# Opening of a macaron transformer layer: fewer warming steps, transfers put behind the opening, and norm steps one pair later

## The chip, the core and the metric

The kernel runs on one core of one Trainium2 chip. The metric is the time of one execution on the device in microseconds (us): the median of three runs of the kernel before is 2084.44 us (2084.19 to 2086.21). The engines are named as the profile names them: PE (TensorE, matmuls), DVE (VectorE), ACT (ScalarE), POOL (GpSimd) and SP (SyncE, which here only issues transfers, each in its turn).

## The reference, cut to what matters

One layer of depth 1 over 1024 latent tokens and 256 context tokens of width 1024. Latent and context rows have their own modulation (nine vectors each, computed from `c` and `c_ctx`), and the same weights.

```python
m_l = jnp.split(silu(c) @ ada_w + ada_b, 9, axis=-1)
m_c = jnp.split(silu(c_ctx)[None] @ ada_w + ada_b, 9, axis=-1)
x   = x   + 0.5 * m_l[2] * swiglu(modulate(rms_norm(x, norm1_w), m_l[0], m_l[1]), w1, w3, w2)
ctx = ctx + 0.5 * m_c[2] * swiglu(modulate(rms_norm(ctx, norm1_w), m_c[0], m_c[1]), w1, w3, w2)
y_l, _ = token_mixing(modulate(rms_norm(x, norm2_w), m_l[3], m_l[4]),
                      modulate(rms_norm(ctx, norm2_w), m_c[3], m_c[4]), ...)
x = x + m_l[5] * y_l
x = x + 0.5 * m_l[8] * swiglu(modulate(rms_norm(x, norm3_w), m_l[6], m_l[7]), ffn2 weights)
return rms_norm(x, final_norm_w)
```

`swiglu` is `(silu(h @ w1) * (h @ w3)) @ w2` with a hidden width of 2816. The change touches the modulation, the first FFN of both streams, and the norm of the latents that follows it.

## The kernel before, in words

Activations lie with the channels on the 128 partitions, in tiles of 512 tokens (latents: groups 0 and 1) or 256 (context: group 2). Each matrix product is made of three fp32r matmuls: an operand is split into a rounded high part and the rest. For a weight tile `raw` the parts are `whi` (written by ACT) and `wlo` (written by DVE, raw minus whi); for activations `hh` and `hl`. In the products of the context FFN the weights are themselves in `hh`/`hl` slots and the hidden values `g` are split into `ghi` and `glo`.

**Opening.** `consts` loads small tables. Then `WARM` matmuls of 128x128 ones (L1970, fp32, each seen as two records) run on an idle psum tile while the first data comes in. After them a `Recorder` notes all work of the opening (context norm, latent norm, first FFN pair); `rec.run()` writes it out in an order that a list scheduler with its own costs finds. All its rows bear line L147. `pe_load(j, hold)` fetches a column group of the modulation's weights (512 KB, `ada<-in_adaN`) for sums on PE; for the very first (j of 8) `hold` makes DVE clear eight columns of the tile, and the transfer waits for that write. After the recorder, plain code follows: `cond_row` fetches the two condition rows (`condc`, and `c_ctx` into a tile named `ada1`, two halves each), ACT takes silu of them, and `mod_load` fetches the other 48 columns (`ada<-in_adaT`, 512 KB each), which DVE multiplies with the rows and reduces (72 reductions, L510) while the rest of the first FFN runs. The scheduler of the framework merges this code into the order of each engine by priority; nothing there ties the fetches on SP to the recorder's end. The silu steps are tied to the recorder's last ACT instruction already.

**Context pairs.** After the first FFN's latent part, `ctx_ffn` makes the second product of the context FFN in 11 pairs of hidden blocks (numbered 0 to 10 below). In pass p of its loop it fetches pair p+2 (`ctx_load`: two halves of `s<-cgd`, four weight tiles `s<-in_w`), splits pair p+1 (`ctx_split`: four hh on ACT, hl on DVE, one of them on POOL, then ghi and glo), makes the 48 matmuls of pair p into psb (`ctx_sums`; "sums p" below), and then takes one step off the list `norms`, which is the latents' second norm cut into steps: column sums of squares on PE (L570) and a power on POOL, the diagonals (`diag1`), the row product on PE and its copy to `nrb` on ACT (`rows1`, L2104), and one step for each of the norm columns (`norm1(k)`: nt on DVE, hh on ACT, hl on DVE; L603, L604, L615). In this region the order on every engine is the program's, into which only work from outside it (the `raw` tiles of the projection that follows, `whi<-raw`) is merged. Tiles of `s` and slots of hh/hl are reused in turn, so a transfer waits for the last reader of the buffer that it takes.

Of the kernel before, what the change touches and what calls it, by code (L numbers as in the profile page):

```python
# [17 lines left out]
P = 128  # L18
D = 1024
KD = D // P  # L20
# [17 lines left out]
SCHED = mybir.DependencyInfo(mybir.DependencyClass.NoSync, mybir.DependencyReason.SCHED_ONLY)  # L38
# [9 lines left out]
class View:  # L48
# [72 lines left out]
    def get(self):  # L121
        t = self.root.real
        for f in self.how:
            t = f(t)
        return t
# [279 lines left out]
class Trunk:  # L405
# [50 lines left out]
    def cond_row(self, name, tag=None):  # L456
        t = self.tile(self.dp, [P, D], F32, tag or "cond" + name)
        for o in (0, 512):
            self.nc.sync.dma_start(t[:, o:o + 512], self.I[name][:, o:o + 512].broadcast_to([P, 512]))
        return t  # L460

    def pe_cond(self, pool):
# [11 lines left out]
        nc.vector.scalar_tensor_tensor(out=self.ab1, in0=self.col("ada_b")[:, 8:16], scalar=1.0, in1=self.col("norm1_w"),  # L474
                                       op0=ALU.add, op1=ALU.mult)

    def pe_load(self, j, hold=False):
        t = self.ada_tile()
        if hold:
            self.nc.vector.memset(t[:, :8], 0.0)  # L480
        self.nc.sync.dma_start(t, self.I["adaN"][PECOL.index(j)])
        return t

# [13 lines left out]

    def mod_load(self, j):
        t = self.ada_tile()
        self.nc.sync.dma_start(t, self.I["adaT"][j])  # L500
        return t

    def mod_col(self, j, ctxs, early=False):
# [625 lines left out]
    def ctx_open(self, xp, n1):  # L1129
        nc, I = self.nc, self.I  # L1130
        a, b = self.mcol(1, 1), self.mcol(0, 1)
        cx = [self.tile(n1, [P, 4 * CTX], F32, f"cx{i}") for i in range(2)]
        for i in range(4):
            nc.sync.dma_start(cx[i // 2][:, i % 2 * 512:i % 2 * 512 + 512], I["ctxP"][:, i * 512:(i + 1) * 512])
        self.ada, self.ab, self.cur = -1, (0, 2, 3, 4, 1), {}
        cur, ws = self.cur, defaultdict(list)
        f32r = lambda pool, tag, bufs=1: tuple(self.tile(pool, [P, 512], F32R, t, bufs) for t in tag)
        slots = iter([*(f"0{k}" for k in range(KD)), *(f"1{k}" for k in range(4, KD))])
        fresh = iter(range(NW))
        raws = iter(range(2 * NW))  # L1140

        def dst(i, q):
            if not q and i < 6:
                return f32r(self.wp, ("whi", "wlo"), NH)
            if not q and i < 11:
                return f32r(self.fp, ("s", "s"), self.ns)
            s = next(slots, None)
            if s:
                return self.hslot(s)
            n = next(fresh)  # L1150
            return f32r(xp, (f"x1{2 * n}", f"x1{2 * n + 1}")) if n < 4 else f32r(self.fp, ("s", "s"), self.ns)

        def half(i, q):
            n = next(raws)
            src = (self.w1, self.w3)[i % 2][i // 2][:, 512 * q:512 * q + 512]
            if n % 2:
                raw = self.tile(xp, [P, 512], F32, f"x0{n // 2 % 8}")
                nc.sync.dma_start(raw, src)
            else:
                raw = self.raw_half(src)  # L1160
            ws[i].append(self.half(raw, dst(i, q)))

        def load(k):
            for j in (8 + k, k):
                cur[j] = self.pe_load(j, j == 8)

        rb = self.ctx_norm(cx, n1, lambda: load(0))
        self.h[2] = []
        hs = [self.hslot(f"1{k}") for k in range(4)]
        csum = lambda n: self.tile(n1, [P, n], F32, "csum", 2)  # L1170

        def norm(k):
            t = cx[k // 4][:, k % 4 * CTX:(k % 4 + 1) * CTX]
            hi, lo = (x[:, k % 2 * CTX:(k % 2 + 1) * CTX] for x in hs[k // 2])
            nc.vector.scalar_tensor_tensor(out=t, in0=t, scalar=a[:, k:k + 1], in1=rb, op0=ALU.mult, op1=ALU.mult)
            nc.scalar.activation(hi, t, AF.Identity, bias=b[:, k:k + 1])
            nc.vector.scalar_tensor_tensor(out=lo, in0=t, scalar=b[:, k:k + 1], in1=hi.bitcast(F32), op0=ALU.add, op1=ALU.subtract)
            self.h[2].append((hi, lo))

        def cols(k):  # L1180
            js = (8 + k, k)
            if k == 0:
                for j in js:
                    p = self.psB()
                    self.col_out(j, self.col_sums(p, 0, j, csum(2 * P)[:, :P], p, P))
                return
            for i, j in enumerate(js):
                self.pe_sums(pc, i * P, cur.pop(j))
            sm = csum(2 * P)
            nc.scalar.copy(sm, pc[:, :2 * P])  # L1190
            src = [self.pe_turn(pc, 2 * P + 2 * i, sm[:, i * P:(i + 1) * P]) for i in range(2)]
            for j, p in zip(js, src):
                self.col_out(j, p)

        cols(0), norm(0)
        pc = self.psB()
        for s in OPEN:
            if isinstance(s, tuple):
                half(*s)
            elif s > 0:  # L1200
                load(s)
            else:
                cols(-s), norm(-s)
        banks = [self.psA() for _ in range(4)] + [self.psB() for _ in range(NW // 2 - 4)]
        acc = [banks[i // 2][:, i % 2 * CTX:(i % 2 + 1) * CTX] for i in range(NW)]
        for k in range(KD):
            for i in range(NW):
                w, h = self.wslice(ws[i], k), self.h[2][k]
                for j, (u, v) in enumerate(((0, 0), (1, 0), (0, 1))):
                    nc.tensor.matmul(acc[i], w[u], h[v], start=k + j == 0 and i % 2 == 0, stop=k == KD - 1 and j == 2,  # L1210
                                     skip_group_check=True)
        return acc
# [730 lines left out]
    def run(self):  # L1943
# [24 lines left out]
        idle = self.psA()  # L1968
        for _ in range(WARM):
            nc.tensor.matmul(idle[:, :P], self.ones, self.ones, start=True, stop=True)  # L1970
        rec = Recorder(self, 0.0, 345e3, 2.0, False)
# [20 lines left out]
        self.h = {tg: get(self.h[tg]) for tg in LATTG}  # L1992
        self.T = [get(t) for t in self.T]
        self.tp = tp.real
        self.cs = [self.cond_row("c"), self.cond_row("c_ctx", "ada1")]
        for t in self.cs:
            for o in (0, 512):
                x = nc.scalar.activation(t[:, o:o + 512], t[:, o:o + 512], AF.Silu)
# [31 lines left out]
        def norm_step(tg, i, a, b):  # L2030
            with self.low(NLOW if tg == 1 and i in (1, 2) else None):
                norm_part(tg, i, a, b)
# [18 lines left out]
        norm2 = lambda tg, i: norm_step(tg, i, self.mcol(4, int(tg == 2)), self.mcol(3, int(tg == 2)))  # L2051
# [33 lines left out]
        def spill(tg):  # L2085
            o = TGS[tg][0]
            for k in range(KD):
                self.nc.sync.dma_start(self.xd[k * P:(k + 1) * P, o:o + 512], self.x[tg][k])
# [4 lines left out]
        def norm1(k):  # L2093
            self.h[1].append(self.hslot(f"1{k}"))
            norm2(1, 3 + k)
# [8 lines left out]
            nc.scalar.copy(nrm[1], pr)  # L2104

        dg = []
        norms = [lambda: norm2(1, 1), diag1, rows1] + [lambda k=k: norm1(k) for k in range(KD - 1)]
        with tc.manual_schedule(engines={mybir.EngineType.PE, mybir.EngineType.DVE, mybir.EngineType.Activation,
                                         mybir.EngineType.Pool, mybir.EngineType.SP}):
            self.ctx_ffn(norms)  # L2110
        norm1(KD - 1)
        spill(1)
        self.lg_start(n2)
        self.psN = self.psB
# [2 lines left out]
        rec = Recorder(self)  # L2117
# [31 lines left out]
        for tg in LATTG:  # L2149
            o, n = TGS[tg]  # L2150
# [57 lines left out]
NQ = 7  # L2208
MB = ((4, 5, 6, 7), (4, 5, 6, 7))
RPRI = 20  # L2210
WARM = 30
NW = 14
F0 = 2
BACKLOG = 3
# [105 lines left out]
```

## Time and profile before

| what | value |
|---|---|
| median of three runs | 2084.44 us |
| the profiled execution's own time | 2084.73 us |
| its span, first to last instruction | 2082.9 us |
| mean granted TensorE clock | 0.995 |
| PE busy | 2067.1 us, 99% |
| DVE, ACT, POOL busy | 1506.3, 987.2, 89.7 us |
| DMA moved | 374.26 MB, mean 180 GB/s |

Times inside the run are counted from the first instruction of the span. A row of the order in time has start, length, engine, line, operation, out<-in with its shape, how many are merged, and in brackets how long the engine was idle before it and what ended that. "PEclk" or "granted clock" is the share of full speed at which TensorE ran.

### The profile page before, as it was taken

The numbers are of one execution on the slowest core, as the hardware profiler recorded it, in microseconds if no ns is written. First come the engines' busy times: TensorE is split into PE (matmuls) and PEld (weight loads), VectorE is DVE, ScalarE is ACT, GpSimd is POOL, SyncE is SP. The second block draws the span as 40 slices with busy tenths as digits, with TensorE's granted clock in tenths as the row PEclk, the third lists the DMA queues.
The fourth block names the chain that finished last, engine by engine and source line by source line (L and its number), as shares of the span: only waits on it lengthen the run. The fifth ranks groups of instructions, "written<-read, shape, count | busy, mean of one in ns | idle before, by whom it ended". The sixth has DMA issues, their size and how long they took to land.

```text
span 2082.9 us, 34381 instructions
## 1 busy us (share of the span) xinstructions
PE 2067.1 (99%) x12438; PEld 1768.0 (85%) x12438; DVE 1506.3 (72%) x2732; ACT 987.2 (47%) x1828; POOL 89.7 (4%) x118
## 2 busy tenths in 40 slices
PE   9999999999999999999999999999999999999998
PEld 8998888888888889998888988888888888888888
DVE  5789999976665688765676478767776666765686
ACT  4665343343444446565575246444434334344553
POOL 0000000000000012001021001000000000010000
PEclk9999999999999999999999999999999999999999
DMA  9863766744488785574232233242344444477674
GB/s 351 276 202 109 248 228 226 267 148 151 142 288 276 268 286 197 175 221 127 80 116 90 82 87 109 88 162 82 112 157 146 146 163 149 159 239 227 219 241 148
DMA packets 207131, 374.26 MB, mean 180 GB/s; under 512 B 23921, under 2 KB 42225, under 8 KB 206833
## 3 DMA queue, kind: packets, MB, share of 16 engines
q1 hardware_dynamic: 206672, 371.94, 53.8%
q8 instruction: 97, 1.59, 0.3%
q14 instruction: 74, 0.60, 0.1%
q10 hardware_dynamic: 288, 0.13, 0.0%
HBM read 293.46 MB, written 70.12 MB: 175 GB/s over the span
## 4 chain that ended last, share of the span: by engine, by line
PE 89%; DMA 5%; DVE 3%; ACT 1%; issue 1%; SPq 0%; DVEq 0%; POOLq 0%; ACTq 0%
PE psa L147 24%; PE psb L147 11%; PE psa L439 9%; PE psa L441 9%; PE psa L440 9%; PE psb L440 8%; PE psb L439 8%; PE psb L441 8%; DMA raw<-in_w 2%; DMA hl<-sd 1%; DMA hl<-in_w 1%; DMA s<-in_w 1%; DVE wlo L435 1%; DMA xd<-x 1%; PE psa L1970 0%
## 5 line engine op out<-in xcount | busy, mean ns | idle before, releaser
L434 ACT ACTIVATE whi<-raw 128x512 fp32r<-128x512 f32 x385 | 243.2, 632 | 552.4 <-issue 190.9
L435 DVE TENSOR_TENSOR wlo<-raw,whi 128x512 fp32r<-128x512 f32 x385 | 264.5, 688 | 209.1 <-ACT whi L434 207.4
L439 PE MATMUL psa<-hh,whi 128*128 128x512 f32 x676 | 263.4, 390 | 0.6 <-ACT s L731 0.6
L441 PE MATMUL psa<-hh,wlo 128*128 128x512 f32 x676 | 263.1, 389 | 0.0
L440 PE MATMUL psa<-hl,whi 128*128 128x512 f32 x676 | 263.0, 389 | 0.0
L147 PE MATMUL psa<-hh,wlo 128*128 128x512 f32 (+1 forms) x664 | 234.5, 353 | 2.3 <-DVE wlo L147 2.3
L147 PE MATMUL psa<-hh,whi 128*128 128x512 f32 (+1 forms) x664 | 234.8, 355 | 0.8 <-ACT hh L147 0.5
L147 PE MATMUL psa<-hl,whi 128*128 128x512 f32 (+1 forms) x664 | 234.1, 353 | 0.0
L440 PE MATMUL psb<-hl,whi 128*128 128x512 f32 x584 | 227.3, 389 | 0.3 <-DVE hl L435 0.3
L439 PE MATMUL psb<-hh,whi 128*128 128x512 f32 x584 | 227.3, 389 | 0.0
L441 PE MATMUL psb<-hh,wlo 128*128 128x512 f32 x584 | 227.2, 389 | 0.0
L147 DVE TENSOR_TENSOR wlo<-raw,whi 128x512 fp32r<-128x512 f32 (+1 forms) x217 | 139.1, 661 | 103.4 <-ACT whi L147 101.5
L147 ACT ACTIVATE whi<-raw 128x512 fp32r<-128x512 f32 (+1 forms) x217 | 129.6, 609 | 151.4 <-PE psa L147 110.5
L439 PEld LDWEIGHTS psa<-hh,whi 128*128 128x128 f32 x676 | 127.0, 188 | 27.1 <-ACT s L731 1.0
L441 PEld LDWEIGHTS psa<-hh,wlo 128*128 128x128 f32 x676 | 126.9, 188 | 26.4
L440 PEld LDWEIGHTS psa<-hl,whi 128*128 128x128 f32 x676 | 126.9, 188 | 26.1
L147 PEld LDWEIGHTS psa<-hh,wlo 128*128 128x128 f32 x664 | 127.2, 192 | 17.3 <-DVE wlo L147 2.5
L147 PEld LDWEIGHTS psa<-hh,whi 128*128 128x128 f32 x664 | 126.9, 191 | 17.6 <-issue 1.0
L147 PEld LDWEIGHTS psa<-hl,whi 128*128 128x128 f32 x664 | 127.1, 192 | 14.7 <-issue 0.2
L440 PEld LDWEIGHTS psb<-hl,whi 128*128 128x128 f32 x584 | 109.6, 188 | 23.2 <-DVE hl L435 0.6
L439 PEld LDWEIGHTS psb<-hh,whi 128*128 128x128 f32 x584 | 109.6, 188 | 23.1 <-ACT hh L434 0.3
L441 PEld LDWEIGHTS psb<-hh,wlo 128*128 128x128 f32 x584 | 109.6, 188 | 22.7
(469 smaller groups left out, 4347.1 us busy)
## 6 DMA issues: line engine op xcount, KB each, us to landing
raw<-in_w SPq DMA_DIRECT2D x316, 256.0 KB, 3.3
gd<-s SPq DMA_DIRECT2D x154, 256.0 KB, 2.9
s<-in_w SPq DMA_DIRECT2D x110, 256.0 KB, 4.5
ada<-in_adaT SPq DMA_DIRECT2D x48, 512.0 KB, 4.7
raw<-gd SPq DMA_DIRECT2D x91, 256.0 KB, 3.4
sd<-s SPq DMA_DIRECT2D x44, 256.0 KB, 2.7
raw<-sd SPq DMA_DIRECT2D x44, 256.0 KB, 3.1
hh<-in_w SPq DMA_DIRECT2D x44, 256.0 KB, 4.0
```

The source lines that it names most:

```text
L147: self.rec.add(self.eng, lambda: f(*map(get, a), **{x: get(v) for x, v in k.items()}), outs, ins, name, a, k)
L434: nc.scalar.activation(hi, src, AF.Copy)
L435: (eng or nc.vector).tensor_tensor(out=lo, in0=src, in1=hi.bitcast(F32), op=ALU.subtract)
L439: mm(ps, wa[0], xa[0], start=start, stop=False, skip_group_check=more)
L440: mm(ps, wa[0], xa[1], start=False, stop=False, skip_group_check=more)
L441: return mm(ps, wa[1], xa[0], start=False, stop=stop, skip_group_check=more)
```

## The change

Three things are changed.

1. `WARM` falls from 30 to 20, and `pe_load` has no `hold` any more: the first column's transfer waits for no write.
2. `cond_row` and `mod_load` tie each of their transfers to the last transfer that the recorder issued on SP (`self.last`): they come behind it in SP's order.
3. The list of norm steps gets an empty first step, and one norm column less; the last two columns are now made after the loop.

```diff
     def cond_row(self, name, tag=None):
...
-            self.nc.sync.dma_start(t[:, o:o + 512], self.I[name][:, o:o + 512].broadcast_to([P, 512]))
+            x = self.nc.sync.dma_start(t[:, o:o + 512], self.I[name][:, o:o + 512].broadcast_to([P, 512]))
+            self.tc.add_manual_dep(x.ins, self.last, SCHED, reason="order")
...
-    def pe_load(self, j, hold=False):
+    def pe_load(self, j):
         t = self.ada_tile()
-        if hold:
-            self.nc.vector.memset(t[:, :8], 0.0)
         self.nc.sync.dma_start(t, self.I["adaN"][PECOL.index(j)])
...
     def mod_load(self, j):
         t = self.ada_tile()
-        self.nc.sync.dma_start(t, self.I["adaT"][j])
+        x = self.nc.sync.dma_start(t, self.I["adaT"][j])
+        self.tc.add_manual_dep(x.ins, self.last, SCHED, reason="order")
...
-                cur[j] = self.pe_load(j, j == 8)
+                cur[j] = self.pe_load(j)
...
         self.tp = tp.real
+        self.last = rec.last["SP"]
         self.cs = [self.cond_row("c"), self.cond_row("c_ctx", "ada1")]
...
-        norms = [lambda: norm2(1, 1), diag1, rows1] + [lambda k=k: norm1(k) for k in range(KD - 1)]
+        norms = [lambda: None, lambda: norm2(1, 1), diag1, rows1] + [lambda k=k: norm1(k) for k in range(KD - 2)]
...
             self.ctx_ffn(norms)
-        norm1(KD - 1)
+        norm1(KD - 2), norm1(KD - 1)
...
-WARM = 30
+WARM = 20
```

SP before, in the first FFN pass of the opening, from 90 us on: weight tiles (`raw<-in_w`), stores of context hidden values (`cgd<-s`), and between them a condition row and columns.

```order
L147 DMA raw_1314<-in_w 128x512
L147 DMA cgd<-s_1262 128x256
L459 DMA ada_542_2695<-in_c_ctx 128x512 x2
L500 DMA ada_632_3166<-in_adaT 128x1024
L147 DMA raw_1371<-in_w 128x512
L500 DMA ada_630_3160<-in_adaT 128x1024
L147 DMA cgd<-s_1369 128x256
L500 DMA ada_631_3163<-in_adaT 128x1024
L147 DMA raw_1436<-in_w 128x512
L147 DMA raw_1458<-in_w 128x512
```

SP now, at the end of the opening: behind its last store (`gd<-s`, the latents' hidden values) stand both condition rows, and then the columns.

```order
L147 DMA gd<-s_2455 128x512
L653 DMA raw_3002<-in_w 128x512
L147 DMA gd<-s_2676 128x512
L459 DMA condc_2681<-in_c 128x512 x2
L459 DMA ada_542_2684<-in_c_ctx 128x512 x2
L499 DMA ada_630_3149<-in_adaT 128x1024
L653 DMA raw_3004<-in_w 128x512
L499 DMA ada_631_3152<-in_adaT 128x1024
```

In the first place the weight tiles now follow each other with only the stores between; the moved ones go some 70 places down. PE before, at the end of sums 0 (`psb<-ghi`, `glo` with hh, hl) and the start of sums 1:

```order
L440 MATMUL psb_7842<-glo_7813,hh_1666_7788 128x256
L441 MATMUL psb_7842<-ghi_7812,hl_1667_7789 128x256
L570 MATMUL psa_7922<-ones_84,nacc_1621_7620 128x1 x4
L439 MATMUL psb_7839<-ghi_7870,hh_1687_7854 128x256
L440 MATMUL psb_7839<-glo_7871,hh_1687_7854 128x256
```

The same place now:

```order
L440 MATMUL psb_7831<-glo_7802,hh_1666_7777 128x256
L441 MATMUL psb_7831<-ghi_7801,hl_1667_7778 128x256
L439 MATMUL psb_7828<-ghi_7859,hh_1687_7843 128x256
L440 MATMUL psb_7828<-glo_7860,hh_1687_7843 128x256
L441 MATMUL psb_7828<-ghi_7859,hl_1688_7844 128x256
```

The four column sums of the norm (L570) have gone behind the 48 matmuls of sums 1. ACT before, from ghi of pair 3 on: the copy of the norm's row, the split of pair 4, then three weight tiles of the projection that follows.

```order
L434 ACTIVATE ghi_8044<-s_7934 128x512
L2104 COPY nrb_8101<-psa_8096 128x512
L434 ACTIVATE hh_1740_8114<-s_8017 128x512
L434 ACTIVATE hh_1742_8118<-s_8018 128x512
L434 ACTIVATE hh_1744_8122<-s_8019 128x512
L434 ACTIVATE hh_1746_8126<-s_8020 128x512
L434 ACTIVATE ghi_8130<-s_8021 128x512
L434 ACTIVATE whi_8747<-raw_8743 128x512
L434 ACTIVATE whi_8771<-raw_8767 128x512
L434 ACTIVATE whi_8890<-raw_8886 128x512
```

ACT now, from the same place (s_7998 to s_8002 are pair 4, s_8085 begins pair 5):

```order
L434 ACTIVATE ghi_8025<-s_7915 128x512
L434 ACTIVATE whi_8736<-raw_8732 128x512
L434 ACTIVATE whi_8760<-raw_8756 128x512
L434 ACTIVATE hh_1738_8096<-s_7998 128x512
L434 ACTIVATE hh_1740_8100<-s_7999 128x512
L434 ACTIVATE hh_1742_8104<-s_8000 128x512
L434 ACTIVATE hh_1744_8108<-s_8001 128x512
L434 ACTIVATE ghi_8112<-s_8002 128x512
L434 ACTIVATE whi_8879<-raw_8875 128x512
L2105 COPY nrb_8169<-psa_8164 128x512
L434 ACTIVATE hh_1755_8182<-s_8085 128x512
```

Two of the three weight tiles have come ahead of pair 4's split, and the third stands ahead of the copy of the row, which is now behind pair 4 and ahead of pair 5. SP now, around the transfer that fills that third tile (raw_8875); cgd and s_8341 to s_8343 are of pair 8, and the buffer of s_8343 is the one that pair 4's glo reads last:

```order
L985 DMA s_8345<-cgd 128x256 x2
L987 DMA s_8341<-in_w 128x512
L987 DMA s_8342<-in_w 128x512
L987 DMA s_8343<-in_w 128x512
L653 DMA raw_8875<-in_w 128x512
L653 DMA raw_8897<-gd 128x512
L653 DMA raw_8899<-in_w 128x512
```

Before, the like transfer (raw_8886) stood one place ahead of the fourth tile of pair 7; it has gone behind three tiles of pair 8, while the stores of the latents that stood ahead of the raw tiles (`xd<-x`, four of them) have gone behind them.

## The prediction

> **What bounds the kernel now.** I read the page's busy table first, then the list of who waited for whom on PE, then a table of stretches around each long wait, then the order of time on ACT, DVE and SP at three places.
>
> ```profile
> PE 2067.1 (99%) x12438; PEld 1768.0 (85%) x12438; DVE 1506.3 (72%) x2732; ACT 987.2 (47%) x1828; POOL 89.7 (4%) x118
> PE psa L147 <- DVE wlo L147: 2.3, 1, 2.3
> PE psa L1970 <- DVE ones L450: 1.0, 1, 1.0
> PE psa L570 <- DVE nacc L561: 1.0, 1, 1.0
> PE psb L440 <- DVE glo L435: 0.2, 1, 0.2
> ```
>
> PE is busy for 2067.1 of 2082.9 us, so only three things can move the time: the few waits of PE, the rate at which its clock runs, and work taken from it. The rows give a wait's total, how often it came, and the longest. The second costs nothing that the change touches; the other three lie in its reach. Next, the stretches (PE busy, matmuls in brackets, then other engines, granted clock, DMA share, GB/s):
>
> ```profile
> 104.90:107.30 2.40, 0.12 (x2) 0.06 (x1) 2.12 (x4) 2.40 (x6) 0.00 (x0) 1.00 0.39 153
> 108.10:111.40 3.30, 3.30 (x18) 3.30 (x17) 2.82 (x5) 0.72 (x1) 0.00 (x0) 0.50 0.54 171
> 111.50:114.90 3.40, 3.40 (x30) 3.40 (x30) 2.88 (x5) 2.83 (x6) 0.00 (x0) 1.00 0.78 257
> 773.70:777.00 3.30, 3.30 (x18) 3.30 (x17) 3.30 (x7) 0.21 (x1) 2.39 (x2) 0.50 1.04 376
> 786.70:792.46 5.76, 5.76 (x51) 5.76 (x50) 4.14 (x6) 4.42 (x9) 1.45 (x1) 1.00 0.97 345
> ```
>
> After each of the two waits (107.25 and 771.89) stands a stretch at half clock. In 3.30 us it passes 18 matmuls; the next row passes 30 in 3.40, so 18 would take 2.04 and a half-clock stretch costs 1.3 us. A wait of PE therefore has a price of its own length plus 1.3.
>
> **Part one, the opening.** The warming steps fall from 30 to 20, and the small DVE write that held the first column's transfer goes.
>
> ```profile
> 1.04 9.14 PE psa L1970 x60
> 7.00:8.00 1.00, 1.00 (x11) 1.00 (x10) 0.25 (x1) 0.20 (x1) 0.00 (x0) 1.00 0.98 377
> 2.00:10.00 8.00, 8.00 (x58) 8.00 (x57) 2.17 (x7) 3.44 (x6) 0.00 (x0) 1.00 0.91 308
> 12.47:15.88 3.41, 2.25 (x42) 1.54 (x32) 2.38 (x6) 2.28 (x6) 0.00 (x0) 1.00 1.03 395
> 15.88:22.71 6.83, 6.79 (x52) 5.22 (x52) 3.94 (x10) 3.60 (x7) 0.00 (x0) 0.50 1.03 405
> ```
>
> Each step is two records (60 for 30). Ten steps fewer are 20 records at 11 to the microsecond: 1.8 to 2.2 us, after which PE takes the sums of squares. But the first FFN matmul then waits for weights: from 12.47 on DMA is full (1.03, 395 GB/s), so weights land earlier only by what the queues gain before. Between 2 and 10 us their share is 0.91, so 8 x 0.09 = 0.7 us of transfer is free there for columns that are issued sooner. I take 1.0, between 0.7 and 2.2 and nearer the first, since the transfers are what PE meets next. Against it stands the clock: half clock begins at 15.88 today, after a stretch in which PE was busy 2.25 of 3.41 us. With the sums ahead by 2 us and the weights by 1, that thin stretch comes earlier, so half clock can begin one stretch earlier, over the first FFN matmuls. Its full price is 1.3, less what waits for weights hide: I take 0.5. Sum: -0.5, ends -2.2 and +1.3.
>
> **Part two, condition rows and columns.** Eight transfers (condc 2, c_ctx 2, four of 512 KB) leave SP between the raw loads of the first FFN pass and go behind the opening's last store.
>
> ```profile
> 100.37 0.64 ACT L147 ACTIVATE whi<-raw 128x512 fp32r<-128x512 f32 x1 [2.60 <-DMA raw<-in_w]
> 103.90 0.63 ACT L147 ACTIVATE whi<-raw 128x512 fp32r<-128x512 f32 x1 [2.63 <-DMA raw<-in_w]
> 104.44 1.32 ACT L147 ACTIVATE hh<-x,mod 128x512 fp32r<-128x512 f32 x2
> 105.18 1.42 DVE L147 SCALAR_TENSOR_TENSOR hl<-x,mod,hh 128x512 fp32r<-128x512 f32 x2 [2.77 <-ACT hh L147]
> 106.51 1.28 DVE L147 TENSOR_TENSOR wlo<-raw,whi 128x512 fp32r<-128x512 f32 x2
> 107.25 0.39 PE L147 MATMUL psa<-hh,wlo 128*128 128x256 f32 x1 [2.28 <-DVE wlo L147]
> ada<-in_adaT SPq DMA_DIRECT2D x4, 512.0 KB, 6.5
> raw<-in_w SPq DMA_DIRECT2D x1, 256.0 KB, 6.1
> raw<-in_w SPq DMA_DIRECT2D x18, 256.0 KB, 3.8
> ```
>
> The last three rows are issues with their median time to landing: the columns from 92 to 104 us, the one raw tile issued between 97.5 and 98, and those from 110 to 135, with no such transfers about. ACT waits for a raw tile twice (the one tile's 97.5 to 98 plus 6.1 is the end of the second wait), and its hh stands behind that; DVE's hl waits for this hh 2.77 us, and the wlo that PE wants stands behind hl. With 3.8 for 6.1 everything from 103.90 on moves up by 2.3. PE, which ran out at 107.25 - 2.28 = 104.97, then has its wlo at 107.25 - 2.3 = 104.95. So the wait falls to about nothing and the half-clock stretch with it: 2.3 + 1.3 = 3.6. Bounds: 1.5 where loads stay bound by their buffers (a wlo of an older tile must free one first), and 4.0 with what little else the queues hold up there.
>
> What the eight meet later:
>
> ```profile
> 215.00:424.00 209.00, 209.00 (x920) 171.92 (x919) 207.90 (x347) 82.35 (x145) 0.00 (x0) 1.00 0.72 242
> L510 DVE CUSTOM_DVE_ANT_0 junk<-ada,condc,cols x48: 1268/1277/1287, 201.8 to 423.7; 128x1024 bf16<-128x1024 f32 x48
> L878 DVE SCALAR_TENSOR_TENSOR x<-s,mod,x x24: 734/744/753, 648.0 to 2048.0; 128x512 f32<-128x512 f32 x24
> ```
>
> The reductions over the columns (72 in all, 1.28 us each) now begin some 12 us later, and end some 15 to 20 later. I cost this at nothing: PE is busy 209.00 of 209.00 there although DVE is at 207.90, DMA has 0.28 free, ACT (82.35 of 209) has room for the four silu of the condition rows, and the gates are first read at 648. If that cover is gone, each microsecond that DVE falls behind PE is one on the end.
>
> **Part three, which the change's words don't name:** a first empty step in the list of norm steps, so that the norm's column sums, the diagonal, the row product and each norm column come one pair of context sums later, and the seventh column after the loop.
>
> ```profile
> 771.89 1.05 PE L570 MATMUL psa<-ones,nacc 128*128 128x1 f32 x8 [1.01 <-DVE nacc L561]
> 772.81 0.36 PE L439 MATMUL psb<-ghi,hh 128*128 128x256 f32 x1
> 786.98 0.59 ACT L2104 COPY nrb<-psa 128x512 f32<-128x512 f32 x1 [5.46 <-PE psa L589]
> 787.47 2.19 ACT L434 ACTIVATE hh<-s 128x512 fp32r<-128x512 f32 x4
> 789.56 0.62 ACT L434 ACTIVATE ghi<-s 128x512 fp32r<-128x512 f32 x1
> 790.08 0.62 ACT L434 ACTIVATE whi<-raw 128x512 fp32r<-128x512 f32 x1
> 791.07 0.63 ACT L434 ACTIVATE whi<-raw 128x512 fp32r<-128x512 f32 x1 [0.37 <-DMA raw<-in_w]
> 790.22 1.52 DVE L435 TENSOR_TENSOR glo<-s,ghi 128x512 fp32r<-128x512 f32 x1 [0.18 <-ACT ghi L434]
> 783.34 0.42 SPq L653 DMA_DIRECT2D raw<-gd  x1
> s<-in_w SPq DMA_DIRECT2D x4, 256.0 KB, 4.1
> raw<-in_w SPq DMA_DIRECT2D x2, 256.0 KB, 6.2
> L615 DVE SCALAR_TENSOR_TENSOR hl<-nt,mod,hh x16: 481/616/754, 793.7 to 862.1; 128x512 fp32r<-128x512 f32 x8, 128x256 fp32r<-128x256 f32 x8
> 835.08 1.26 DVE L978 SCALAR_TENSOR_TENSOR x<-psb,mod,x 128x256 f32<-128x256 f32 x3
> ```
>
> (The two issue rows are of 788.5 to 793.7 and of 785.2 to 786.5.) What it gains: the wait of 1.01 at 771.89, its half-clock stretch 1.3, and perhaps the 0.2 on glo: 2.5. What is late next: PE now runs sums 1 straight on from 770.9. At 5.76 each (the row of 786.70), with 0.9 for the column sums (771.89 to 772.81) and 0.8 for the row product (eight records at 0.1, as in the warming), it wants sums 4 at 789.9 and sums 5 at 795.7. The order on ACT has changed too: two whi<-raw now stand ahead of pair 4's split, and a third ahead of the copy of nrb, behind which stand the four hh and the ghi of pair 5. On SP the raw tile of that third whi stands behind the last weight tile of pair 8, and that tile takes the buffer that pair 4's glo frees. So a loop goes from glo of pair 4 to glo of pair 5: two issues 0.5, landing 4.1, whi 0.5, copy 0.5, four hh 2.1, ghi 0.6, glo 1.5, in all 9.8 us, where PE has 5.76.
>
> When is glo of pair 4 done? The raw tiles were issued from 783.3 on, and the second landed at 791.0, since the whi of 791.07 waited for it. Four stores and some four tile loads that stood ahead now stand behind, at 256 KB / 345 GB/s = 0.76 each 6 us, and sums 1 free their buffers 1.9 sooner (770.9 for 772.8), so it lands at about 783; then whi 0.5 and, as before, 4.3 from the first hh (787.47) to the end of glo (791.74), plus some 0.7 for a wlo now ahead of it on DVE: 788.5. Glo of pair 5 is then done at 798.3, and PE, which wants it at 795.8, waits 2.5, with a half-clock stretch behind it: 3.8. Ends of the wait: 0 with a landing of 3.8 and glo of pair 4 at 786 (its buffers come free as sums 2 end, 783.3), 6 with a landing of 6.2 and glo at 790. At the loop's end DVE does three norm columns instead of two ahead of the rows that empty psb at 835.08: 0.7 for hl (0.75 for 512 columns in its row), as much for nt, and a wait for ACT between, 2.1 at most; PE overwrites psb right behind, so 0 to 2.1, I take 0.7. Part three: -2.5 + 3.8 + 0.7 = +2.0, ends -2.5 and +7.
>
> **The sum.** -0.5 - 3.6 + 2.0 = -2.1 on the profiled execution's 2084.73 us (span 2082.9 and 1.8 around it): 2082.6. That run lies 0.3 above the median of the runs, 2084.44, so I forecast 2082.3.
>
> **The clock rule weighed.** Both waits of PE, 2.28 and 1.01, were followed by half clock. [...]
>
> **Rivals.** (1) The loop finds slack: the raw tile lands in 3.8 and pair 4 splits early, so part three keeps its 2.5: -0.5 - 3.6 - 2.5 = -6.6, 2077.8. For it: fewer stores crowd the queues. Against it: SP's order, which ties that load to glo. 17%. (2) Slower: the same loop with a landing of 6.2 and pair 4 late, a wait of 6 with two half-clock stretches (2.6): part three is -2.5 + 8.6 + 0.7 = +6.8, the sum +2.7 and 2087.1. It passes zero where the wait exceeds 4.6 us. For it: 6.2 is measured there; against: with the stores moved the queues are shorter. 8%. (3) Part two does little, because loads wait for their buffers: 2.1 us less gain, 2084.4; SP's waits for wlo speak for it, the clear fall from 6.1 to 3.8 against. 9%. (4) The opening loses: half clock one stretch longer, +1.3 for -0.5: 2084.1; 9%. (5) Half clock follows longer idleness only, so that no wait costs more than itself: 2083.6 by the sum above; the two rows at 0.50 speak against it, 2%. My forecast: 55%, with a range of its own of 2080.3 to 2084.3.
>
> **Chances.** 0.2% of 2084.44, 4.2 us, is about what a measurement can tell from no change; faster begins at 2080.3. That is rival 1 and about a sixth of my forecast's case: 26%. Slower (from 2088.6) is a part of rival 2 and mishaps: 5%. The rest, 69%, is within it. The range reaches from inside rival 1 to just past 2084.4.
>
> **What would show it.** Right: no wait at about 105 and no half clock behind it; no wait of L570; a new wait of PE on ghi or glo, 2 to 3 us, at about 792 (795.8 less what parts one and two save), with ACT waiting for a raw tile just ahead of the copy of nrb. Wrong: if that copy runs without a wait for DMA, part three pays in full; if the first FFN matmul comes later than 15.50, the opening loses; a wait of PE between 200 and 640 would mean that the moved columns are not covered.

## The result, and the profile after

The changed kernel is slower: a ratio of 1.0028 to the kernel before, 95% interval 1.0019 to 1.0037 (medians 2091.98 and 2085.99 us, 16 executions each), which is 5.8 us where 2.1 us less were forecast. The profiled execution took 2088.59 us (span 2086.8 us, granted clock 0.997).

The busy table and the list of PE's waits after the change (total, how often, longest):

```profile
PE 2063.8 (99%) x12418; PEld 1764.2 (85%) x12418; DVE 1505.5 (72%) x2731; ACT 987.6 (47%) x1828; POOL 92.6 (4%) x118
PE psb L439 <- ACT ghi L434: 3.8, 1, 3.8
PE psa L439 <- ACT s L704: 2.3, 3, 1.4
PE psb L440 <- DVE glo L435: 1.8, 2, 1.2
PE psb L439 <- DVE s L872: 1.3, 1, 1.3
```

The waits that the prediction set out to remove are gone: none for wlo (2.28) and none for nacc at L570 (1.01). In their place stand the wait for ghi, larger than forecast, one of 1.2 for glo right behind it, and two groups that had no price in the prediction's sum: PE waits for psa behind ACT (s, L704) between 200 and 450 us, and once for psb behind DVE (s, L872) at 763.

The same stretches as before, in the trace after:

```profile
2.00:10.00 8.00, 8.00 (x46) 7.55 (x44) 2.16 (x6) 3.44 (x6) 0.00 (x0) 1.00 0.97 335
15.88:22.71 6.83, 6.55 (x69) 5.41 (x70) 4.63 (x10) 3.51 (x7) 0.00 (x0) 1.00 1.03 397
104.90:107.30 2.40, 2.40 (x22) 2.40 (x21) 2.40 (x5) 0.86 (x2) 0.00 (x0) 1.00 0.77 229
215.00:424.00 209.00, 207.02 (x909) 169.65 (x908) 204.76 (x342) 80.03 (x142) 0.00 (x0) 1.00 0.72 241
798.43:805.26 6.83, 5.68 (x27) 5.62 (x27) 6.60 (x9) 3.54 (x7) 2.17 (x2) 0.50 0.85 272
```

The opening and the place of the old stall run at full clock here (third column from the right 1.00, where 15.88 to 22.71 had 0.50), and DMA is fuller between 2 and 10 us (0.97 for 0.91). Between 215 and 424 PE is no longer busy throughout: 207.02 of 209, and DVE fell with it, 204.76 for 207.90. At 798 stand two half-clock stretches on end (6.83 us at 0.50).

Where the time went can be followed by setting the n-th matmul of PE behind the warming beside the n-th of the other trace (between 209 and 454 us some of them come in another order, of which more below). After is ahead of before by 1.8 us at the sums of squares, 3.5 at 22 us and 7.7 at 111; the lead falls to 3.9 at 440 and 2.2 at 763, rises to 5.0 at 777, where the wait of L570 was, and at 806, behind the half clock, after is 3.8 us behind, 3.9 at the end. This compares one execution with one; the experiments show how much of it every execution has.

### The profile page after: what moved, and what is told of

The parts are those of the page before. It is cut to its first block, busy times and chain, and to the rows that moved or that the text cites. A ratio compares the mean times of both kernels' runs of the same rounds, so it can differ in the third digit from the quotient of the medians.

```text
span 2086.8 us, 34331 instructions
## 1 busy us (share of the span) xinstructions
PE 2063.8 (99%) x12418; PEld 1764.2 (85%) x12418; DVE 1505.5 (72%) x2731; ACT 987.6 (47%) x1828; POOL 92.6 (4%) x118
## 4 chain that ended last, share of the span: by engine, by line
PE 88%; DVE 5%; DMA 2%; ACT 2%; issue 2%; SPq 0%; DVEq 0%; POOLq 0%; ACTq 0%
PE psa L147 23%; PE psb L147 10%; PE psa L439 9%; PE psa L440 9%; PE psa L441 9%; PE psb L441 8%; PE psb L439 8%; PE psb L440 8%; DVE junk L510 1%; DVE wlo L435 1%; DMA s<-in_w 1%; DMA hl<-sd 0%; DMA raw<-in_w 0%; PE psa L1970 0%; DMA s<-cgd 0%
## 5 line engine op out<-in xcount | busy, mean ns | idle before, releaser
L440 PE MATMUL psa<-hl,whi 128*128 128x512 f32 x676 | 263.4, 390 | 0.0
L440 PE MATMUL psb<-hl,whi 128*128 128x512 f32 x584 | 227.5, 389 | 0.0
L440 PEld LDWEIGHTS psa<-hl,whi 128*128 128x128 f32 x676 | 127.0, 188 | 26.0
L440 PEld LDWEIGHTS psb<-hl,whi 128*128 128x128 f32 x584 | 109.7, 188 | 22.7
```

The source lines that it names most:

```text
L440: mm(ps, wa[0], xa[1], start=False, stop=False, skip_group_check=more)
```

## The experiments

Theory 1, formed on these two traces: parts one and two gain what they take off the opening and the stall at 105; part of it is given back between 200 and 450 because the condition rows and columns now come late; and part three costs more than it gains, because on ACT a third whi, whose raw tile is fetched late, stands ahead of the copy of nrb and of pair 5's split. Theory 2: the waits between 200 and 450 come from a PE that is ahead of a full DVE, wherever the columns stand. Theory 3: the wait at 798 comes from PE's earliness or crowded transfers, not from part three.

The ratios are of executions taken in turn with the kernel before on the same chip. A ratio of 0.0010 is 2.1 us. Apart from the change itself, the kernels were timed in three rounds, each on another chip: rows 1 to 4; rows 6 to 8; rows 9 to 12. Rows of different rounds are compared through their ratios alone.

| kernel | ratio to before | 95% interval | in us |
|---|---|---|---|
| part one alone | 0.9995 | 0.9987 to 1.0004 | -1.0 |
| part two alone | 1.0005 | 0.9995 to 1.0014 | +1.0 |
| part three alone | 1.0035 | 1.0023 to 1.0047 | +7.3 |
| parts one and two | 1.0002 | 0.9993 to 1.0010 | +0.4 |
| the change (all three) | 1.0028 | 1.0019 to 1.0037 | +5.8 |
| parts one and two, columns earlier | 0.9986 | 0.9977 to 0.9996 | -2.9 |
| the change, later fetch | 1.0007 | 0.9997 to 1.0017 | +1.5 |
| the change, columns earlier, later fetch | 0.9991 | 0.9981 to 1.0000 | -1.9 |
| part three alone, later fetch | 1.0013 | 1.0003 to 1.0023 | +2.7 |
| parts one and two, columns earlier, later fetch | 0.9979 | 0.9969 to 0.9989 | -4.4 |
| part two alone, columns earlier | 0.9981 | 0.9970 to 0.9991 | -4.0 |
| the change, both, and two norm columns in one step | 0.9991 | 0.9982 to 1.0000 | -1.9 |

**Part one alone.** The opening's edits on the kernel before.

```diff
-        if hold:
-            self.nc.vector.memset(t[:, :8], 0.0)
-WARM = 30
+WARM = 20
```

> Part one alone on the kernel before: 20 warming steps, first column's transfer waits for no write; the eight transfers and the norm steps stay as before. Theory 1 (late columns): PE runs 3 to 3.5 us ahead of before from 22 us to 104 us, the stall at about 105 with its half clock stays or grows by part of the lead (loads there are bound by the transfers), and no new waits of 0.5 us or more come between 200 and 450, since the columns come as early as before: net 0 to -3.5 us, about -2. Theory 2 (DVE is full there, and a PE that is ahead must wait whatever comes late): waits of 0.5 us or more on psa between 200 and 450 as in the changed kernel, summing to the lead, net about 0. Theory 3 (the wait at 798 comes from PE's earliness): a wait on ghi of 2 us or more at 780 to 800.

Measured: ratio 0.9995 (0.9987 to 1.0004), the gain within what the measurement can tell. In its trace PE is 3.6 us ahead from 22 to 102 us, its mean granted clock is 0.998 (0.995 in the first trace of before), and the stall at 105 is 1.3 us, where theory 1 expected it to stay or grow. Its waits, from the list:

```profile
PE psa L568 <- DVE nacc L559: 1.4, 1, 1.4
PE psa L147 <- DVE wlo L147: 1.3, 1, 1.3
PE psb L439 <- DVE s L870: 1.1, 1, 1.1
```

No wait stands between 200 and 450 although PE is 6.3 us ahead there. That speaks against theory 2. The wait on DVE's s at 760 (L870 here is L872 of the changed kernel) is here too, without any moved column or norm step. Its trace ends 4.8 us ahead, far more than the ratio gives: this profiled execution, 2079.91 us, is the fastest of the 11.

**Part two alone.** The order only.

```diff
+        self.last = rec.last["SP"]
...
+            self.tc.add_manual_dep(x.ins, self.last, SCHED, reason="order")
```

> Part two alone on the kernel before: condition rows and columns tied behind the opening's last transfer; opening and norm steps as before. Theory 1: the stall at 105 and its half clock go, about -4.2 us at 111; then about 3.6 us are lost again between 200 and 450 in waits of PE for psa behind ACT silu and DVE reductions, as in the changed kernel; net 0 to -1 us by 700, no wait of 3 us at 798. Theory 2: the same waits, but fewer, 1 to 2 us, since PE is ahead by less than in the changed kernel. Theory 3: a wait on ghi of 2 us or more at 780 to 800.

Measured: 1.0005 (0.9995 to 1.0014), +1.0 us where 0 to -1 were expected, within what the measurement can tell. In the trace PE is 5.3 us ahead at 111 and 1.8 at 441: 3.5 us are given back, as theory 1 said. PE's waits between 200 and 450:

```profile
PE psa L439 <- ACT s L706: 1.9, 2, 1.0
PE psb L441 <- DVE wlo L435: 0.3, 1, 0.3
```

The same waits as in the changed kernel, with PE less far ahead: theory 2's "fewer" can't be told from theory 1 by this run, but by the next pair.

**Part two alone, but tied to the 150th transfer of the recorder instead of the last.** In the trace the first condition row is then issued at 157.28 us; with the columns behind the last transfer it was 204.10.

```diff
+        if key == "SP":
+            self.names.append(x.ins.name)
...
-        self.last = rec.last["SP"]
+        self.last = rec.names[149]
```

> Part two alone, but tied to the 150th transfer of the recorder instead of the last. If lateness costs what the two orders with parts one and two differ by (0.16%, 3 us): no wait of 0.5 us or more between 200 and 450, DVE busy about 221 of 224 us between 200 and 424 (212 with the columns behind the last transfer), median 2 to 4 us under part two alone, 1 to 3 under before. If not: as part two alone.

Measured: 0.9981 (0.9970 to 0.9991), against 1.0005 (0.9995 to 1.0014) with the columns last; the intervals don't meet, and 0.0024 is 5.0 us (2 to 4 were expected). The stall at 105 is gone all the same; the ten microseconds around it, in this trace:

```profile
100.00:110.00 10.00, 10.00 (x86) 10.00 (x85) 9.03 (x16) 5.65 (x11) 0.00 (x0) 1.00 0.64 203
```

What lateness does is read from one stretch, 200 to 424 us (PE busy, PEld, DVE, ACT, POOL, clock, DMA). Before:

```profile
200.00:424.00 224.00, 224.00 (x985) 184.13 (x984) 222.87 (x372) 88.53 (x156) 0.00 (x0) 1.00 0.72 241
```

Part two alone, with its columns behind the last transfer:

```profile
200.00:424.00 224.00, 222.12 (x974) 181.67 (x973) 212.34 (x354) 88.41 (x156) 0.00 (x0) 1.00 0.73 244
```

And tied to the 150th:

```profile
200.00:424.00 224.00, 224.00 (x985) 184.18 (x984) 222.26 (x370) 87.36 (x153) 0.00 (x0) 1.00 0.73 241
```

DVE does 10 us less there when the columns are late (212.34 for 222.87), though it is nearly full in the kernel before, and PE stands for 1.9. With the earlier place both are as before. Most of what DVE misses lies at the start: between 200 and 216 us it is busy 8.95 of 16 us with the late columns, 15.96 in the kernel before and 15.93 with the earlier place; at the other end, between 424 and 445, it is busy 20.87 of 21 where the kernel before has 15.52. The start is seen in the changed kernel on ACT, around 207 us, and in the group of reductions (durations in ns, then first and last start):

```profile
207.15 1.33 ACT L1999 ACTIVATE condc<-condc 128x512 f32<-128x512 f32 x2 [2.03 <-DMA condc<-in_c]
209.41 0.63 ACT L1999 ACTIVATE ada<-ada 128x512 f32<-128x512 f32 x1 [0.93 <-DMA ada<-in_c_ctx]
209.95 0.62 ACT L434 ACTIVATE whi<-raw 128x512 fp32r<-128x512 f32 x1
212.03 0.56 ACT L704 COPY s<-psa 128x512 f32<-128x512 f32 x1
```

```profile
L510 DVE CUSTOM_DVE_ANT_0 junk<-ada,condc,cols x48: 1270/1279/1289, 215.3 to 441.2; 128x1024 bf16<-128x1024 f32 x48
```

The silu of the condition rows waits for its transfers on ACT (2.03 and 0.93), and behind it in ACT's order stand a whi and the copy that empties psa. The reductions begin at 215.3 for 201.8 and the last starts at 441.2 for 423.7. PE is hit by both, but not equally. Behind the silu it waits 0.33 at 212.65 in the changed kernel, and not at all there in part two alone. Its larger waits come later (0.58 at 251.82 and 1.40 at 368.35; in part two alone 1.05 at 254.29 and 0.83 at 370.28), and there ACT stands for 3.5 us until DVE, busy without a gap (3.50 of the 3.50 us from 363.2 in the changed kernel), has made an `s`, with the copy that empties psa behind it. The last of them in the changed kernel:

```profile
366.67 0.63 ACT L731 ACTIVATE s<-s 128x512 f32<-128x512 f32 x1 [3.51 <-DVE s L708]
367.73 0.57 ACT L704 COPY s<-psa 128x512 f32<-128x512 f32 x1
368.35 0.50 PE L439 MATMUL psa<-hh,whi 128*128 128x512 f32 x1 [1.40 <-ACT s L704]
```

One thing more changed with the place. Between about 200 and 454 us the traces with the columns behind the last transfer have another order on PE, DVE and ACT than the kernel before (294 of PE's matmuls stand at another place); those with the earlier place, or with part two left out, have the order of before. So the 5.0 us belong to the place of the transfers together with the order that the framework's scheduler makes of it; no run separates the two.

**Parts one and two together, and the same with the earlier place.** The second differs from the first by the diff just shown.

> Parts one and two together, the norm steps as before. Theory 1: -7.7 us at 111, about 3.6 lost again between 200 and 450, some 1.7 at 763 where the first product of the context waits for DVE, no wait of 3 us at 798, but the wait of 1.0 on nacc at 770 with its half clock still there; net -2 to -3 us. Theory 2: the same to 700. Theory 3: a wait on ghi of 2 us or more at 780 to 800, net +2 us or more.

> Parts one and two without part three, but the condition rows and columns are tied to the 150th of the recorder's transfers on SP (issued at about 160 us) instead of its last one (about 209). Theory 1 (late columns cost waits between 200 and 450): no silu waits for a condition row behind 200 us, no wait of 0.5 us or more between 200 and 450 from reductions that bunch, 2 us less in the trace by 450 than with parts one and two; median 1 to 3 us under before. Theory 2 (PE ahead of a full DVE): the waits stay, the same time as parts one and two, within 1 us of before.

Measured: 1.0002 (0.9993 to 1.0010) and 0.9986 (0.9977 to 0.9996), 3.3 us apart, in the direction of theory 1 again; the intervals overlap a little. In the first trace no wait of PE stands at 763 and only one between 200 and 450 (0.9, behind L704), so the trace lost 1.3 us there where 3.6 was expected, and yet the ratio shows no gain where 2 to 3 us were expected: a miss of that expectation. In the second none of PE's waits lies between 200 and 450. In neither is there a wait of 2 us at 798: theory 3 falls. A third pair that differs by the place alone stands further down, both timed in one round: the change with the later fetch (1.0007) and the same with the columns earlier (0.9991), 3.3 us apart.

**Part three alone.**

```diff
-        norms = [lambda: norm2(1, 1), diag1, rows1] + [lambda k=k: norm1(k) for k in range(KD - 1)]
+        norms = [lambda: None, lambda: norm2(1, 1), diag1, rows1] + [lambda k=k: norm1(k) for k in range(KD - 2)]
```

> Part three alone on the kernel before: the empty first norm step, and the seventh column behind the loop; opening and transfers as before. Theory 1: to 770 us as before; the wait of L570 and its half clock go (-2.5), and waits of 3.5 to 5 us in all on ghi and glo come at 795 to 805, with half clock behind them, because the third whi ahead of the copy of nrb waits for its raw tile: net +4 to +6 us. Theory 3 (earliness or crowded transfers): no such wait, net -2.5 us.

Measured: 1.0035 (1.0023 to 1.0047), 7.3 us, where 4 to 6 were expected: by itself somewhat more than the whole change. Its waits between 760 and 850:

```profile
PE psb L439 <- ACT ghi L434: 3.8, 1, 3.8
PE psb L439 <- DVE s L872: 1.7, 1, 1.7
PE psb L440 <- DVE glo L435: 0.9, 1, 0.9
PE psb L439 <- DVE x L978: 0.8, 1, 0.8
```

The same wait of 3.8 as in the changed kernel, at the opening and transfers of before. How it comes about, in order of time, first on ACT, then DVE, then SP:

```profile
786.23 0.63 ACT L434 ACTIVATE whi<-raw 128x512 fp32r<-128x512 f32 x1 [0.72 <-DMA raw<-in_w]
786.76 2.18 ACT L434 ACTIVATE hh<-s 128x512 fp32r<-128x512 f32 x4
788.84 0.62 ACT L434 ACTIVATE ghi<-s 128x512 fp32r<-128x512 f32 x1
798.25 0.63 ACT L434 ACTIVATE whi<-raw 128x512 fp32r<-128x512 f32 x1 [8.79 <-DMA raw<-in_w]
798.78 0.57 ACT L2104 COPY nrb<-psa 128x512 f32<-128x512 f32 x1
799.25 2.19 ACT L434 ACTIVATE hh<-s 128x512 fp32r<-128x512 f32 x4
801.34 0.62 ACT L434 ACTIVATE ghi<-s 128x512 fp32r<-128x512 f32 x1
...
791.54 0.68 DVE L435 TENSOR_TENSOR glo<-s,ghi 128x512 fp32r<-128x512 f32 x1
...
792.98 0.42 SPq L653 DMA_DIRECT2D raw<-in_w  x1
```

The split of pair 4 starts at 786.76, behind the second whi, whose tile landed at 786.2. Its glo is done at 792.2 (791.54 + 0.68); only then does SP reach the raw tile (792.98), which lands 5.3 later at 798.25; and ACT, idle for 8.79 us, still has copy, four hh and ghi ahead of what PE wants.

**The change with the fetch one pair later.** The raw tiles of the projection that follows may start in pass 4 of `ctx_ffn` instead of 3; the copy of nrb and pair 5's split then come ahead of the third whi.

```diff
-            if p == 3:
+            if p == 4:
                 self.gate = self.begun.ins.name
```

> The changed kernel with one number more changed: the weight tiles of the projection that follows may be fetched one pair later (pass 4 instead of 3), so that on ACT the third whi no longer stands ahead of the copy of nrb and of the split of pair 5. Theory 1 (the loop through that tile makes the wait): no wait of 2 us or more on ghi or glo between 780 and 810 and no half clock there; the norm steps cost no more than 1 us; median 6 to 8 us under the changed kernel, within 2 of before. Rival (the later norm itself makes PE wait, or transfers are crowded there): a wait of 2 us or more stays, the median within 3 us of the changed kernel.

Measured: 1.0007 (0.9997 to 1.0017) for 1.0028 (1.0019 to 1.0037), 4.4 us less; 6 to 8 were expected. The wait of 3.8 is gone, as theory 1 said, and a later one took part of its place. Its waits, and DVE at the end of the loop:

```profile
PE psb L439 <- DVE x L978: 2.3, 1, 2.3
PE psb L439 <- DVE s L872: 1.7, 1, 1.7
PE psb L440 <- DVE glo L435: 1.1, 2, 0.6
```

```profile
830.27 0.75 DVE L603 SCALAR_TENSOR_TENSOR nt<-x,mod,nrb 128x512 f32<-128x512 f32 x1
831.80 0.75 DVE L615 SCALAR_TENSOR_TENSOR hl<-nt,mod,hh 128x512 fp32r<-128x512 f32 x1 [0.79 <-ACT hh L604]
...
834.88 1.26 DVE L978 SCALAR_TENSOR_TENSOR x<-psb,mod,x 128x256 f32<-128x256 f32 x3
```

The third norm column behind the loop holds DVE from 830.27 to 832.5 (2.2 us) ahead of the reads that empty psb, and PE waits 2.27, with a half-clock stretch behind it (0.50 from 835.80 to 839.18). In the changed kernel the same 2.2 us cost only 0.25, since PE had already stood for 5 us at 798: one wait covered the other.

**Part three alone with the later fetch.** The same line on the kernel with part three alone.

> Part three alone with the later fetch of the following projection's tiles (pass 4 for 3); opening and transfers as before. If the wait of 3.8 came from that tile and the third norm column behind the loop costs 2 us at 835: no wait over 1.5 at 780 to 810, one of about 2 us on psb behind DVE at 835, no wait on nacc at 770; within 2 us of before, 5 to 8 under part three alone. If the later norm steps cost by themselves: 4 us or more over before.

Measured: 1.0013 (1.0003 to 1.0023), 4.6 us under part three alone, 2.7 over before. Its waits between 760 and 850:

```profile
PE psb L439 <- DVE x L978: 1.5, 1, 1.5
PE psb L440 <- DVE glo L435: 1.3, 1, 1.3
PE psb L439 <- DVE s L872: 1.2, 1, 1.2
PE psb L439 <- ACT ghi L434: 0.8, 1, 0.8
```

So the tile made most of the loss, not all of it: without it the later norm steps still cost some 3 us, of which the wait behind L978 is the one that was expected. The expectation (within 2 us of before, 5 to 8 under part three alone) was missed by a little, and the intervals of the two kernels just meet at 1.0023.

**All three parts with both mends, and with two norm columns in one step.**

```diff
-        norms = [...] + [lambda k=k: norm1(k) for k in range(KD - 2)]
+        norms = [...] + [lambda k=k: [norm1(i) for i in k] for k in ((0,), (1,), (2,), (3, 4), (5,), (6,))]
...
-        norm1(KD - 2), norm1(KD - 1)
+        norm1(KD - 1)
```

> All three parts with both mends: condition rows and columns tied to the 150th transfer of the recorder, and the fetches of the following projection one pair later. Theory 1: no wait over 1 us between 100 and 760 nor at 780 to 810, no wait on nacc at 770; median 2 to 6 us under before (2079 to 2083). Theory 2 or the rival above: at or above before.

> All three parts with both mends, and one middle step of the norm list makes two columns, so that two instead of three columns lie between the last glo and the reads that empty psb. If the third column makes the wait of 2.3 at 835: that wait and its half clock are gone or under 0.5, at the price of up to 0.7 in the middle; median 1 to 4 us under the kernel with three columns there (0.9991 of before). If the wait stays at 2 us, it comes from the raw tiles that DVE splits there.

Measured: 0.9991 (0.9981 to 1.0000) and 0.9991 (0.9982 to 1.0000), -1.9 us both, where 2 to 6 under before and then 1 to 4 less were expected. The first has the wait of 2.3 behind DVE's x; in the second it is gone, which shows that the third column made it, but PE waits elsewhere (line numbers are three higher in this kernel: L443 for L440, L875 for L872):

```profile
PE psb L443 <- DVE glo L438: 2.5, 2, 1.3
PE psb L442 <- DVE s L875: 1.1, 1, 1.1
```

The two waits for glo stand at 798.7 (1.28) and at 818.9 (1.18), the second behind the step with two columns. DVE's work there was moved, not saved, and the time is the same.

**Without part three: parts one and two, columns earlier, later fetch.**

> Parts one and two with the earlier place for columns (the 150th transfer), the norm steps as before, and the later fetch of the following projection's tiles. The wait on nacc at 770 (1.4) with its half clock stays; the waits on glo and ghi at 793 to 796 (1.5 together in the trace without the later fetch) go if those tiles make them, and no wait of 2 us comes at 835, since only two norm columns lie there. Median 0 to 2 us under the kernel without the later fetch (0.9986 of before). If the two versions agree within 1 us, that fetch matters only where the copy of the norm's row stands behind it.

Measured: 0.9979 (0.9969 to 0.9989), 4.4 us under before, and the best of all here beside part two alone with the earlier place (0.9981). Against the same kernel without the later fetch (0.9986) it is 1.5 us, less than the intervals can tell, though the wait for glo at 795 of that kernel's trace (1.28) is 0.16 here. With part three the same two mends stood at 0.9991, 2.5 us more, with intervals that overlap.

**The kernel before once more.** A second trace of the kernel before, unchanged.

> The kernel before, unchanged, for a second trace of it. If the waits and half-clock stretches of the first trace are what every execution has, it shows the wait of 2.28 at 107.25, that of 1.01 at 771.89, and half clock at about 16 to 22.7, 108 and 774. If they come by chance, some of these are missing: the mean granted clock over the runs of before is 0.9966, where the profiled one had 0.995, so I expect about one half-clock stretch of 3.4 us less.

Measured: one execution of 2090.69 us. The expectation of less half clock was wrong (mean clock 0.995 as in the first trace). Its longest waits:

```profile
PE psa L570 <- DVE nacc L561: 1.4, 1, 1.4
PE psa L147 <- ACT whi L147: 1.4, 1, 1.4
PE psb L440 <- DVE glo L435: 1.3, 1, 1.3
PE psb L439 <- DVE s L872: 1.1, 1, 1.1
```

The stall of 2.28 at the end of the first FFN pass is here too (at 108.56), and the wait of L570. But three waits of over 1 us are here that the first trace of the same kernel did not have, the one behind DVE's s (at 769) among them. So what the changed kernel lost at 763, a wait of 1.3, need not come from the change: the kernel before has it in one of its two traces.

## Why the prediction was wrong, point by point

- **Part one (forecast -0.5, ends -2.2 and +1.3).** Alone it measured -1.0, interval -2.7 to +0.8: the size holds as far as it can be told. The first FFN matmul came 1.4 to 2.0 us earlier in the traces of part one, of parts one and two and of the change (13.69 in the changed kernel, 15.50 before), where 1.0 was taken on the reading that it waits for weights. In the trace of before its wait (0.55 us, to 15.50) is for ACT's hh, which hangs on PE's own sums of squares, so it moves up by what PE gains there, 1.8 in the change. The rest of the 3.5 us that the trace shows is half clock: the opening had 6.83 us of it in the first trace of before (0.50 from 15.88 to 22.71) and none in the changed kernel's (1.00 there). One pair of traces doesn't tell how much of that comes with the 20 steps: single executions of the kernel before had mean clocks of 0.995 to 0.999.
- **Part two, the stall (forecast -3.6).** The mechanism was right: without the eight transfers among the raw loads the wait at 105 is gone in every kernel that has the order, and with the moved columns kept early the part measures -4.0 (-6.3 to -1.9).
- **Part two, the moved columns: the first step that failed.** "I cost this at nothing" was wrong by 5.0 us, more than the part gains. PE's 209.00 of 209 us beside DVE's 207.90 were read as cover; DVE's row said that there was little. DVE, that full, made up nothing of the delay of its input: the reductions began 13.5 us later in the change and the last started 17.5 later, where the prediction put the delay at 12 and 15 to 20. It also named the price ("each microsecond that DVE falls behind PE is one on the end") without asking whether it would fall due; as a price that was too high, since DVE did 10 us less there and PE lost 3. It counted ACT's room for the four silu (82.35 of 209 busy), but not that ACT's copies, which empty psa, stand in order behind steps that wait, for the silu's transfers (0.33 us of PE's waits in the change) and above all for the late DVE (0.58 and 1.40). Nor did it ask whether the other order that comes with the move has a price. The sign named for it, a wait of PE between 200 and 640, is what the trace shows.
- **Part three (forecast +2.0, ends -2.5 and +7): the second step that failed.** Alone it measured +7.3 (+4.8 to +9.8), just above the end of +7. The place and the loop were right: ACT waits for the third raw tile ahead of the copy of nrb. The wait was mis-sized, 2.5 for 4.7 (3.76 and 0.94 in part three alone, 3.76 and 1.15 in the change), and brought half clock for two stretches, not one (6.82 us at 0.50 in part three alone, 6.83 in the change). Two terms were off. The start of the loop: the second raw tile was put at about 783, on the argument that fewer stores stand ahead, and landed at 786.2; so glo of pair 4 came at 792.2 for 788.5. PE was late as well, and wanted sums 5 at 798.25 (802.01 - 3.76) for 795.8, so that of these 3.7 us some 1.3 count. The loop itself: it took 5.3 from issue to landing for 4.1, 11.3 in all for 9.8, and closed at 803.5 (801.99 + 1.49) for 798.3. This is rival 2 (8%), whose price for part three was +6.8. The term for psb (0.7, ends 0 and 2.1) measured 0.25 in the change and 0.80 in part three alone, where PE was late anyway, and 2.27 with the later fetch, where it was not.
  The terms as measured in its trace, -2.5 + 4.7 + 2.6 + 0.8, give +5.6; what makes the rest is not shown. A wait of 1.7 at 767 behind DVE's s stands in that trace too, but one of that kind is also in the second trace of the kernel before.
- **The sum.** Against -2.1 for the whole, 5.8 came. The parts as measured alone give -1.0 + 1.0 + 7.3 = +7.3, which agrees with +5.8 (+4.0 to +7.7) within their intervals. Against the forecasts that is -0.5 for part one, +4.6 for part two and +5.3 for part three.
- **The half-clock price (1.3 each).** Taken as certain behind each wait, which the runs don't bear out: a wait of 1.01 us had half clock behind it, one of 1.4 and one of 2.28 had none (below). The fifth rival's 2083.6 counts each wait at its own length instead, -0.5 - 2.3 + 2.0 = -0.8; no run shows a length of idleness from which half clock follows.

## What to carry to other kernels

A stage in which two engines are both full has little cover: a delayed input can be paid there (here 5.0 us, with PE at 209.00 and DVE at 207.90 of 209), also through a third engine whose order puts one engine's work behind the other's. Ask for the latest place that still feeds the full engine in time: here 47 us earlier was early enough. And look at what a tie does to the orders of the other engines. Where a step is put later in a hand-written order, follow the loop that its new neighbour closes (buffer, issue, landing, split) with measured landings, and ask which wait stands behind the one that you remove, because a long wait hides the next (here 0.25 us was left behind one of 3.76, and 2.27 came where that one was gone). One trace against one trace misleads on small edits: time the parts alone.

## What the runs showed of the hardware

Half clock came in stretches of 3.41 us (from 108.03 and from 773.63 in the first trace of before) and of 6.83 us (from 15.88 there, from 798.43 in the changed kernel), the one at the end of each kernel apart, and not behind each wait. The wait of L570 (0.9 to 1.4 us) stands in eight traces. Behind that of 1.01 in the first trace of before PE runs at 0.50 from 773.63; behind that of 1.4 in the second the clock stays at 1.00, in the stretches that hold it and follow it:

```profile
773.40:776.80 3.40, 2.06 (x18) 1.85 (x16) 3.09 (x5) 1.78 (x3) 0.00 (x0) 1.00 0.85 240
776.90:780.20 3.30, 3.30 (x28) 3.30 (x29) 2.24 (x5) 0.00 (x0) 2.00 (x2) 1.00 1.04 372
```

The stall of 2.28 has it behind it in the first trace of before; in part three alone with the later fetch the same stall does not, in the stretches that hold it and follow it:

```profile
101.30:104.60 3.30, 1.02 (x9) 0.82 (x8) 2.07 (x4) 3.30 (x7) 0.00 (x0) 1.00 0.69 255
104.70:108.00 3.30, 3.30 (x28) 3.30 (x29) 3.30 (x6) 0.96 (x2) 0.00 (x0) 1.00 0.65 193
```

PE is busy for 1.02 of 3.30 us and the clock stays at 1.00, where before, with the same stall, 3.30 us behind it passed 18 matmuls at 0.50. So the length of a wait alone doesn't give its price; what else decides is not shown.

The clock is also a part of what part three costs. Its five executions had a mean granted clock of 0.9952, the kernel before beside them 0.9966; over a span of 2085 us the difference is 2.9 us of full speed, or some 2 to 3 of the 7 us between their means. That the rest is waits is inferred, not measured.
